# One factor for the two norms in front of a gated layer, and accumulators of their own per token tile in the last half of a down projection

## The chip, the cores and the metric

The kernel runs on one core of a Trainium2 chip. The metric is device time in microseconds, the median of several runs. TensorE is called PE (its weight loads are PEld), VectorE DVE, ScalarE ACT, GpSimd POOL; SyncE (SP) issues the transfers of the weights.

## What is computed

The input is 256 tokens of 1024 columns in float32. Two transformer blocks follow each other. The first is a mixer with sparse attention and an MLP with squared ReLU, and it ends with a norm; the second is a gated layer, a second mixer and a gated layer again. Cut to the part around the change:

```python
def rmsnorm(x, g):
    xf = x.astype(jnp.float32)
    y = xf * lax.rsqrt(jnp.mean(xf * xf, axis=-1, keepdims=True) + EPS)
    return (y * g.astype(jnp.float32)).astype(x.dtype)
...
x = rmsnorm(x, norm_final)                  # end of the first block
f = swiglu(rmsnorm_2(x, ffn1_pre_g[l]), ffn1_w_gate[l], ffn1_w_up[l], ffn1_w_down[l])
x = x + 0.5 * rmsnorm_2(f, ffn1_post_g[l])
```

So two norms stand right behind each other between the MLP's output (x2 in the kernel) and the products with the gate and up weights. The output of the first of them is also the residual of the gated layer.

## The kernel before

Every product runs in float32 as three matmuls of rounded parts: both operands are split into a rounded part (hi) and a residual (lo). The weights are streamed in units of 128x1024 values: SP transfers a unit (line 246), ACT writes hi (line 262), DVE writes lo = raw - hi (line 263). The split runs two units ahead of PE, the transfer five.

Products come in two kinds. `gemm_pair` (lines 358 to 376) computes a chunk of 256 features for all tokens: the features lie on the partitions, 16 pairs of a 512 column matmul (line 368) and a 256 column one (line 369) fill a pair of PSUM banks; ACT copies one half out (line 373), DVE adds the other (line 374) into a tile `sum`, of which there are two. `gemm_tok` (lines 287 to 335) computes 512 output columns (a column half) for two token tiles of 128 tokens, with the tokens on the partitions (lines 305 to 307), and calls `done` for each token tile when its last matmul has been issued. In the MLP and the gated layers PSUM holds three accumulator tiles of two banks each, and two banks for transposes; there, with `pair` set, the two token tiles of a chunk are the two banks of one accumulator tile. In the mixers every token tile has a tile of one bank.

The last column half of a down projection is called with `tail=2` (line 1160, in `down_post`): the last two units are first run for token tile 0 to the end, then for token tile 1, so that what follows for token tile 0 (a square with its sum, the gain on line 1123, a root, the new residual on line 1140) runs beside the matmuls of token tile 1.

`mlp` (lines 1008 to 1064) computes the MLP's chunks, then the two column halves of its output. `odone` (line 1036) adds the residual on line 1039, which gives x2, and squares it on ACT (`ssq`, line 432). The transposed parts of x2, times both gains by column (`gg`), are made by jobs (`jx`, lines 399 to 403) that go on between matmuls; the factor of the norm is left out of them and multiplied in later. Behind the column halves come the sum of the squares (line 1048), its mean, and an inverse root by Newton steps (lines 434 to 445) that gives rf; then xf = x2 * rf * gain (line 1057) in two passes, the squares of xf, a second mean and inverse root, and the product of both factors, rs (line 1063).

`ffn` (lines 1165 to 1187) spreads rs along the tokens (`along_free`, lines 538 to 551: two scalings of ones on line 547, matmuls on line 548, a copy to rsB on line 549), and multiplies rsB into each chunk of the gate product (line 1178) ahead of the SiLU (line 1179).

The order on PE, ACT and DVE is not that of the text: a planner with a timeline of its own lays it out when the program is built. SP and POOL work in the order of the text. The pools of `mlp` (`mlph`, `mlpt`) are given back at the end of the `with` block, and the gated layer's pools take their space.

Of the kernel before, what the change touches and what calls it, by code (L numbers as in the profile page):

```python
# [9 lines left out]
F32 = mybir.dt.float32  # L10
# [4 lines left out]
ALU = mybir.AluOpType  # L15
# [6 lines left out]
D = 1024  # L22
KT = 2
NEG = -1.0e30
EPS = 1e-6
# [184 lines left out]
class Prog:  # L210
# [76 lines left out]
    def gemm_tok(self, W, c, xh, xl, done, head=0, tail=0, mid=None, late=None, rate=1, delay=0, acc=None):  # L287

        nc = self.nc
        w = W.widths[c]
        if self.pair:
            ps = self.pacc.tile([128, 2, 512], F32, tag="acc", name="acc")
            ps = [ps[:, 0, :], ps[:, 1, :]]
        else:
            acc = acc or (lambda: self.pacc.tile([128, 512], F32, tag="acc", name="acc"))
            ps = [acc() for _ in range(2)]
        nu = len(W.off[c])

        def mm(kt, t):
            k, hi, lo = kt
            sl = slice(t * 128, t * 128 + 128)
            last = k == W.kt - 1
            nc.tensor.matmul(ps[t][:, :w], xh[:, k, sl], hi, start=(k == 0), stop=False)  # L305
            nc.tensor.matmul(ps[t][:, :w], xh[:, k, sl], lo, start=False, stop=False)  # L306
            nc.tensor.matmul(ps[t][:, :w], xl[:, k, sl], hi, start=False, stop=last)  # L307
            if last:
                done(t, ps[t][:, :w])

        held = []
        for u in range(nu):
            kts = self.load_unit(W, c, u)
            if u < head or u >= nu - tail:
                for kt in kts:
                    mm(kt, 0)
                    if u < head:
                        self.flush(rate)
                held += kts
                if u == head - 1 or u == nu - 1:  # L320
                    if u == head - 1 and mid:
                        mid()
                    for i, kt in enumerate(held):
                        mm(kt, 1)
                        if u < head:
                            self.flush(rate)
                        elif late:
                            late(len(held) - 1 - i)
                    held = []
                continue  # L330
            for kt in kts:
                for t in range(2):
                    mm(kt, t)
                if delay <= kt[0] < W.kt - 1:
                    self.flush(rate)
# [672 lines left out]
    def mlp(self, x1):  # L1008
        tc, nc, g = self.tc, self.nc, self.g
        s = self.small(2, "s1")  # L1010
        for t in range(2):
            self.ssq(s[:, t:t + 1], x1[:, t, :])
        r2 = self.small(2, "r1")
        self.mean_eps(r2, s)
        nc.vector.reciprocal(r2, r2)
        x2 = self.xp.tile([128, 2, D], F32, tag="x", name="x2")
        sq = self.small(4, "s2")
        gg = self.small(8, "gg")
        nc.vector.tensor_tensor(gg, g["norm_final"], g["ffn1_pre_g_2"], op=ALU.mult)
        with tc.tile_pool(name="mlph", bufs=1) as hp, tc.tile_pool(name="mlpt", bufs=2) as tp:  # L1020
            hT = [hp.tile([128, 32, 256], F32R, name="hT%d" % i) for i in range(2)]

            self.sump = tp

            def hdone(c):
                def f(p):
                    h = tp.tile([128, 2, 256], F32, tag="h", name="h")
                    nc.vector.scalar_tensor_tensor(h, p, 0.0, p, op0=ALU.max, op1=ALU.mult)
                    self.split_sb(h, hT, 2 * c)
                return f  # L1030
            for c in range(len(W_MI.widths)):
                self.gemm_pair(W_MI, c, self.x1T, hdone(c), delay=1, rate=2)
            xT = self.new_xT()
            jx = self.split_T(lambda t, k: x2[:, t, k * 128:k * 128 + 128], range(8), [0, 1], *xT, gg)

            def odone(c):
                def f(t, ps):
                    cs = slice(c * 512, c * 512 + 512)
                    nc.vector.scalar_tensor_tensor(x2[:, t, cs], ps, r2[:, t:t + 1], x1[:, t, cs], op0=ALU.mult,
                                                   op1=ALU.add)  # L1040
                    self.ssq(sq[:, 2 * c + t:2 * c + t + 1], x2[:, t, cs])
                return f
            for c in range(2):
                self.gemm_tok(W_MO, c, *hT, odone(c), delay=1, rate=2)
                self.later(*jx[4 * c:4 * c + 4])
        self.dump("x2", x2)
        ss = self.small(2, "s2b")
        nc.vector.tensor_tensor(ss, sq[:, 0:2], sq[:, 2:4], op=ALU.add)
        v = self.small(2, "vf")
        self.mean_eps(v, ss)  # L1050
        rf = self.small(2, "rf")
        self.newton_rsqrt(rf, v, 2, "rfn")
        gf = self.row_gain(0)
        xf = self.xp.tile([128, 2, D], F32, tag="x", name="xf")
        s = self.small(2, "sf")
        for t in range(2):
            nc.vector.scalar_tensor_tensor(xf[:, t, :], x2[:, t, :], rf[:, t:t + 1], gf, op0=ALU.mult, op1=ALU.mult)
            self.ssq(s[:, t:t + 1], xf[:, t, :])
        v2 = self.small(2, "vf2")
        self.mean_eps(v2, s)  # L1060
        rs = self.small(2, "rsf")
        self.newton_rsqrt(rs, v2, 2, "rsn")
        nc.vector.tensor_tensor(rs, rs, rf, op=ALU.mult)
        return xf, xT, rs

    def split_sb(self, h, hT, k):

# [508 lines left out]
```

## Time and profile before

| | us |
|---|---|
| median of 3 runs | 1151.42 |
| lowest and highest | 1150.39, 1152.96 |
| profiled execution | 1152.25 |
| its span, first to last instruction | 1150.5 |
| PE busy | 1114.8 (97%) |
| DVE busy | 769.6 (67%) |
| ACT busy | 573.0 (50%) |
| POOL busy | 137.0 (12%) |

Times in the rows are microseconds from the span's start. In a timeline a row is: start, duration, engine, line of the kernel, operation, written tile <- read tiles, shape, count, and in brackets the idle time of the engine just before it with what ended it. PE's rows are pipelined: a matmul starts before the one ahead of it has ended, so that what counts is the distance from start to start. The MLP's output projection ends near 414, the first gated layer runs from about 409 to 609, the last one to the end.

### The profile page before, as it was taken

What the parts mean: (1) busy time and instruction counts of PE and PEld (TensorE: products, weight loads), DVE (VectorE), ACT (ScalarE), POOL (GpSimd) and SP (SyncE); (2) the same over time, 40 slices, a digit from 0 to 9 for tenths busy, and PEclk for the clock granted to TensorE, in tenths of its full rate; (3) what the DMA queues carried; (4) which work ended last, traced back from release to release, by engine and by line L of the source; (5) the groups of instructions that cost most, each with busy time, mean ns of one, the idle gap of its engine ahead of it and who ended that gap; (6) DMA issues with size and microseconds to landing.
All of it is one profiled execution on the core that took longest, in us unless ns stands there. A gap on an engine that the chain in (4) does not pass through costs nothing.

```text
span 1150.5 us, 17641 instructions
## 1 busy us (share of the span) xinstructions
PE 1114.8 (97%) x6848; PEld 995.0 (86%) x6848; DVE 769.6 (67%) x1207; ACT 573.0 (50%) x854; POOL 137.0 (12%) x141
## 2 busy tenths in 40 slices
PE   8988999999999998999999999999999999999997
PEld 8877899888888877888878999889999987888885
DVE  6855776777754466776547686556779777777643
ACT  6424454465544455555445334544555555655552
POOL 1411220000000000000000675000323000000000
PEclk9998999999999998999999999999999999999999
DMA  8782114666555654555554655434545555555552
GB/s 295 250 193 94 63 53 143 201 185 198 185 193 175 202 174 153 183 183 188 196 178 146 209 179 167 166 129 143 174 148 167 159 190 178 186 189 189 183 183 74
DMA packets 55876, 196.91 MB, mean 171 GB/s; under 512 B 6700, under 2 KB 6972, under 8 KB 55536
## 3 DMA queue, kind: packets, MB, share of 16 engines
q1 hardware_dynamic: 52704, 186.44, 49.6%
q0 software_dynamic: 2800, 9.21, 3.2%
q8 instruction: 54, 0.88, 0.3%
q14 instruction: 30, 0.25, 0.1%
q10 hardware_dynamic: 288, 0.14, 0.0%
HBM read 192.84 MB, written 1.44 MB: 169 GB/s over the span
## 4 chain that ended last, share of the span: by engine, by line
PE 84%; POOL 5%; DMA 4%; DVE 4%; ACT 2%; issue 1%; DVEq 0%; SPq 0%; POOLq 0%; ACTq 0%
PE acc L368 19%; PE acc L369 10%; PE acc L305 9%; PE acc L306 9%; PE acc L307 9%; PE acc L349 6%; PE acc L351 6%; PE acc L352 6%; PE sm L835 2%; POOL sw L1255 2%; DMA sw<-qkT 2%; POOL qkT L1256 2%; DMA BT<-tvd 1%; PE o L868 1%; POOL qkT L1254 1%; DVE lo L263 1%
## 5 line engine op out<-in xcount | busy, mean ns | idle before, releaser
L263 DVE TENSOR_TENSOR lo<-raw,hi 128x1024 fp32r<-128x1024 f32 (+2 forms) x356 | 450.7, 1269 | 270.9 <-ACT hi L262 268.9
L262 ACT ACTIVATE hi<-raw 128x1024 fp32r<-128x1024 f32 (+2 forms) x356 | 371.1, 1044 | 439.1 <-issue 132.7
L368 PE MATMUL acc<-xs,hi 128*128 128x512 f32 x960 | 342.6, 401 | 6.2 <-DVE sum L374 6.0
L369 PE MATMUL acc<-xs,lo 128*128 128x256 f32 x960 | 270.1, 282 | 0.7 <-DVE lo L263 0.7
L368 PEld LDWEIGHTS acc<-xs,hi 128*128 128x128 f32 x960 | 181.9, 190 | 50.5 <-issue 4.7
L349 PE MATMUL acc<-xs,hi 128*128 128x256 f32 (+1 forms) x696 | 199.7, 288 | 0.3 <-ACT hi L262 0.3
L351 PE MATMUL acc<-xs,hi 128*128 128x256 f32 (+1 forms) x696 | 198.9, 287 | 0.0
L352 PE MATMUL acc<-xs,lo 128*128 128x256 f32 (+1 forms) x696 | 198.0, 287 | 0.1
L369 PEld LDWEIGHTS acc<-xs,lo 128*128 128x128 f32 x960 | 182.9, 191 | 1.3 <-DVE lo L263 1.0
L349 PEld LDWEIGHTS acc<-xs,hi 128*128 128x128 f32 (+1 forms) x696 | 133.4, 192 | 3.7 <-issue 2.5
L351 PEld LDWEIGHTS acc<-xs,hi 128*128 128x128 f32 (+1 forms) x696 | 133.7, 192 | 2.4 <-issue 2.0
L352 PEld LDWEIGHTS acc<-xs,lo 128*128 128x128 f32 (+1 forms) x696 | 132.9, 192 | 1.6 <-issue 1.0
L305 PE MATMUL acc<-hi,hT 128*128 128x512 f32 x304 | 118.7, 391 | 3.4 <-DVE f L1123 3.4
L306 PE MATMUL acc<-lo,hT 128*128 128x512 f32 x304 | 118.5, 390 | 0.0
L307 PE MATMUL acc<-hi,hT 128*128 128x512 f32 x304 | 118.0, 389 | 0.0
L305 PEld LDWEIGHTS acc<-hi,hT 128*128 128x128 f32 x304 | 57.1, 188 | 16.1 <-DVE f L1123 4.3
L307 PEld LDWEIGHTS acc<-hi,hT 128*128 128x128 f32 x304 | 57.1, 188 | 11.9
L306 PEld LDWEIGHTS acc<-lo,hT 128*128 128x128 f32 x304 | 57.1, 188 | 11.7
L305 PE MATMUL acc<-hi,xs 128*128 128x386 f32 (+1 forms) x128 | 48.6, 381 | 2.1 <-DVE xs L403 2.0
L306 PE MATMUL acc<-lo,xs 128*128 128x386 f32 (+1 forms) x128 | 48.2, 377 | 0.0
L307 PE MATMUL acc<-hi,xs 128*128 128x386 f32 (+1 forms) x128 | 47.3, 376 | 0.0
L374 DVE TENSOR_TENSOR sum<-acc,sum 128x512 f32<-128x512 f32 x60 | 41.1, 684 | 0.0
(419 smaller groups left out, 1388.2 us busy)
## 6 DMA issues: line engine op xcount, KB each, us to landing
raw<-in_w_in SPq DMA_DIRECT2D x100, 512.0 KB, 3.5
raw<-in_ffn_w_gate SPq DMA_DIRECT2D x44, 512.0 KB, 3.4
raw<-in_ffn_w_up SPq DMA_DIRECT2D x44, 512.0 KB, 3.4
raw<-in_ffn_w_down SPq DMA_DIRECT2D x44, 512.0 KB, 3.4
raw<-in_w_mlp_in SPq DMA_DIRECT2D x32, 512.0 KB, 3.5
raw<-in_w_mlp_out SPq DMA_DIRECT2D x32, 512.0 KB, 3.3
raw<-in_w_out SPq DMA_DIRECT2D x16, 512.0 KB, 3.4
raw<-in_w_in SPq DMA_DIRECT2D x16, 386.0 KB, 3.5
```

The costliest lines, as they stand in the source:

```text
L262: nc.scalar.activation(hi[:, :n * w], raw[:, :n * w], AF.Copy)
L263: nc.vector.tensor_tensor(lo[:, :n * w], raw[:, :n * w], hi[:, :n * w], op=ALU.subtract)
L305: nc.tensor.matmul(ps[t][:, :w], xh[:, k, sl], hi, start=(k == 0), stop=False)
L306: nc.tensor.matmul(ps[t][:, :w], xh[:, k, sl], lo, start=False, stop=False)
L307: nc.tensor.matmul(ps[t][:, :w], xl[:, k, sl], hi, start=False, stop=last)
L349: nc.tensor.matmul(o, hi[:, fs], xh[:, k, :], start=(k == 0 and f % 2 == 0), stop=False, skip_group_check=True)
L351: nc.tensor.matmul(o, hi[:, fs], xl[:, k, :], start=False, stop=False, skip_group_check=True)
L352: nc.tensor.matmul(o, lo[:, fs], xh[:, k, :], start=False, stop=last, skip_group_check=True)
L368: nc.tensor.matmul(ps[:, f, :, :], hi[:, fs], x.both[:, k, :, :], start=(k == 0), stop=False)
L369: nc.tensor.matmul(ps[:, f, 0, :], lo[:, fs], x.hi[:, k, :], start=False, stop=last)
L374: nc.vector.tensor_tensor(s, ps[:, :, 0, :], s, op=ALU.add)
L835: nc.tensor.matmul(ps[:, i, :], q[pr:pr + 64, U["fts"][i], t * 128:t * 128 + 128], kk, start=True, stop=True)
```

## The change

`gemm_tok` with `pair` and `tail` takes two accumulator tiles instead of one; each token tile then has the first bank of a tile of its own.

In `mlp` the row of gains is fetched ahead of the column halves. `odone` also multiplies x2 by the gain on POOL, into a new tile of the MLP's pool, and squares that product on ACT. Behind the column halves the sums of both kinds of squares give both factors: with v the mean of x2's squares plus EPS and w the mean of the product's squares, the product of the two old factors is one inverse root, of w + EPS * v. It comes first; rf, the inverse root of v, comes second and scales the product (in two passes on DVE, with a column of factors) to the residual that the gated layer adds at its end.

```diff
--- before.py
+++ after.py
@@ -291,8 +291,8 @@
         nc = self.nc
         w = W.widths[c]
         if self.pair:
-            ps = self.pacc.tile([128, 2, 512], F32, tag="acc", name="acc")
-            ps = [ps[:, 0, :], ps[:, 1, :]]
+            ps = [self.pacc.tile([128, 2, 512], F32, tag="acc", name="acc") for _ in range(2 if tail else 1)]
+            ps = [ps[0][:, 0, :], ps[1][:, 0, :] if tail else ps[0][:, 1, :]]
         else:
             acc = acc or (lambda: self.pacc.tile([128, 512], F32, tag="acc", name="acc"))
             ps = [acc() for _ in range(2)]
@@ -1036,32 +1036,38 @@
             def odone(c):
                 def f(t, ps):
                     cs = slice(c * 512, c * 512 + 512)
+                    i = 2 * c + t
                     nc.vector.scalar_tensor_tensor(x2[:, t, cs], ps, r2[:, t:t + 1], x1[:, t, cs], op0=ALU.mult,
                                                    op1=ALU.add)
-                    self.ssq(sq[:, 2 * c + t:2 * c + t + 1], x2[:, t, cs])
+                    nc.gpsimd.tensor_tensor(xf[:, t, cs], x2[:, t, cs], gf[:, cs], op=ALU.mult)
+                    self.ssq(sq[:, i:i + 1], x2[:, t, cs])
+                    self.ssq(sy[:, i:i + 1], xf[:, t, cs])
                 return f
+            gf = self.row_gain(0)
+            xf = hp.tile([128, 2, D], F32, name="xg")
+            sy = self.small(4, "s3")
             for c in range(2):
                 self.gemm_tok(W_MO, c, *hT, odone(c), delay=1, rate=2)
                 self.later(*jx[4 * c:4 * c + 4])
+
+
+            v = self.small(2, "vf")
+            nc.vector.tensor_tensor(v, sq[:, 0:2], sq[:, 2:4], op=ALU.add)
+            self.mean_eps(v, v)
+            v2 = self.small(2, "vf2")
+            nc.vector.tensor_tensor(v2, sy[:, 0:2], sy[:, 2:4], op=ALU.add)
+            w2 = self.small(2, "vf3")
+            nc.vector.tensor_scalar(w2, v, EPS, None, op0=ALU.mult)
+            nc.vector.scalar_tensor_tensor(v2, v2, 1.0 / D, w2, op0=ALU.mult, op1=ALU.add)
+            rs = self.small(2, "rsf")
+            self.newton_rsqrt(rs, v2, 2, "rsn")
+            rf = self.small(2, "rf")
+            self.newton_rsqrt(rf, v, 2, "rfn")
+            xo = self.xp.tile([128, 2, D], F32, tag="x", name="xf")
+            for t in range(2):
+                nc.vector.tensor_scalar(xo[:, t, :], xf[:, t, :], rf[:, t:t + 1], None, op0=ALU.mult)
         self.dump("x2", x2)
-        ss = self.small(2, "s2b")
-        nc.vector.tensor_tensor(ss, sq[:, 0:2], sq[:, 2:4], op=ALU.add)
-        v = self.small(2, "vf")
-        self.mean_eps(v, ss)
-        rf = self.small(2, "rf")
-        self.newton_rsqrt(rf, v, 2, "rfn")
-        gf = self.row_gain(0)
-        xf = self.xp.tile([128, 2, D], F32, tag="x", name="xf")
-        s = self.small(2, "sf")
-        for t in range(2):
-            nc.vector.scalar_tensor_tensor(xf[:, t, :], x2[:, t, :], rf[:, t:t + 1], gf, op0=ALU.mult, op1=ALU.mult)
-            self.ssq(s[:, t:t + 1], xf[:, t, :])
-        v2 = self.small(2, "vf2")
-        self.mean_eps(v2, s)
-        rs = self.small(2, "rsf")
-        self.newton_rsqrt(rs, v2, 2, "rsn")
-        nc.vector.tensor_tensor(rs, rs, rf, op=ALU.mult)
-        return xf, xT, rs
+        return xo, xT, rs
 
     def split_sb(self, h, hT, k):
 
```

## Rows read from the trace of the kernel before

**Rows 1.** Page: the span, and PE's busy time.
```profile
span 1150.5 us, 17641 instructions
...
PE 1114.8 (97%) x6848; PEld 995.0 (86%) x6848; DVE 769.6 (67%) x1207; ACT 573.0 (50%) x854; POOL 137.0 (12%) x141
```

**Rows 2.** PE's timeline at the start of the first gated layer.
```profile
416.77 0.39 PE L369 MATMUL acc<-xs,lo 128*128 128x256 f32 x1 [0.69 <-DVE lo L263]
...
428.13 0.28 PE L369 MATMUL acc<-xs,lo 128*128 128x256 f32 x1
...
429.99 0.50 PE L368 MATMUL acc<-xs,hi 128*128 128x512 f32 x1 [1.58 <-DVE sum L374]
...
441.70 0.28 PE L369 MATMUL acc<-xs,lo 128*128 128x256 f32 x1
...
446.39 0.77 PE L368 MATMUL acc<-xs,hi 128*128 128x512 f32 x1 [4.42 <-DVE sum L374]
...
452.27 0.39 PE L368 MATMUL acc<-xs,hi 128*128 128x512 f32 x1
...
452.62 0.40 PE L368 MATMUL acc<-xs,hi 128*128 128x512 f32 x1
```

**Rows 3.** Busy time by stretch; after the POOL columns granted clock, DMA share, GB/s.
```profile
450.00:452.00 2.00, 2.00 (x7) 1.69 (x7) 0.90 (x2) 0.33 (x1) 0.00 (x0) 0.50 0.00 0
```

**Rows 4.** DVE's timeline at the start of the first gated layer.
```profile
414.40 0.75 DVE L1039 SCALAR_TENSOR_TENSOR x<-acc,r,x 128x512 f32<-128x512 f32 x1 [0.22 <-PE acc L307]
...
415.49 1.23 DVE L263 TENSOR_TENSOR lo<-raw,hi 128x1024 fp32r<-128x1024 f32 x1 [0.34 <-ACT hi L262]
...
423.11 0.15 DVE L445 SCALAR_TENSOR_TENSOR rf<-rfn_t,rf 128x2 f32<-128x2 f32 x1
...
423.30 2.48 DVE L1057 SCALAR_TENSOR_TENSOR xf<-x,rf,row 128x1024 f32<-128x1024 f32 x2
...
433.63 0.16 DVE L1063 TENSOR_TENSOR rsf<-rsf,rf 128x2 f32<-128x2 f32 x1
...
435.24 0.48 DVE L547 TENSOR_SCALAR rt<-ones,rsf 128x128 f32<-128x128 f32 x2
...
439.81 0.42 DVE L549 COPY rsB<-tr 128x256 f32<-128x256 f32 x1 [1.67 <-PE tr L548]
```

**Rows 5.** ACT's timeline at the start of the first gated layer.
```profile
415.37 0.61 ACT L432 ACTIVATE junk<-x 128x512 bf16<-128x512 f32 x1
...
424.68 1.06 ACT L432 ACTIVATE junk<-xf 128x1024 bf16<-128x1024 f32 x1 [2.00 <-DVE xf L1057]
...
427.91 0.58 ACT L373 ACTIVATE sum<-acc 128x512 f32<-128x512 f32 x1
...
444.92 0.60 ACT L373 ACTIVATE sum<-acc 128x512 f32<-128x512 f32 x1
```

**Rows 6.** Timeline, last half of the first gated layer's down projection.
```profile
602.14 0.39 PE L307 MATMUL acc<-hi,hT 128*128 128x512 f32 x1
...
603.45 0.74 DVE L1123 SCALAR_TENSOR_TENSOR f<-acc,rsf,row 128x512 f32<-128x512 f32 x1
...
604.25 0.50 PE L305 MATMUL acc<-hi,hT 128*128 128x512 f32 x1 [1.73 <-DVE f L1123]
```

**Rows 7.** Timeline, last half of the last gated layer's down projection.
```profile
1138.56 0.39 PE L307 MATMUL acc<-hi,hT 128*128 128x512 f32 x1
...
1140.67 0.50 PE L305 MATMUL acc<-hi,hT 128*128 128x512 f32 x1 [1.72 <-DVE f L1123]
```

**Rows 8.** Timeline, last half of the mixer's output projection.
```profile
948.66 0.68 DVE L1121 TENSOR_TENSOR f<-acc,row 128x512 f32<-128x512 f32 x1
948.80 0.39 PE L306 MATMUL acc<-lo,mT 128*128 128x512 f32 x1
```

**Rows 9.** Timeline, POOL and DVE beside each other in the mixer.
```profile
858.70 1.29 POOL L1448 TENSOR_TENSOR qkm<-xc,y 128x512 f32<-128x512 f32 x1
...
858.85 1.16 DVE L443 TENSOR_TENSOR h_t<-h0r 128x4 f32<-128x4 f32 x1
```

## The prediction

> **What bounds the kernel now.** The page comes first: the span is 1150.5 us, and TensorE (PE) is busy for 97% of it [rows 1]. An edit can then only gain where PE stands still or runs slowly. So the second view is PE's own timeline at the two places that the change touches, the start of the first gated layer and the last column half of a gated layer's down projection; the reader is to look for the brackets, which give idle time and what ended it. The third view is the DVE and ACT timelines beside those stops.
>
> At the start of the gated layer PE stops three times [rows 2]. The first stop is a wait for a weight residual, 0.69 us at 416.77. The second runs from the end of the matmul that starts at 428.13 to 429.99. A pair of matmuls (512 and 256 columns) starts every 0.35 us at full pace (452.27, 452.62), of which the narrow one has a third, 0.12; so the stop is 429.99 - 428.13 - 0.12 = 1.74 us. The third is 446.39 - 441.70 - 0.12 = 4.57 us. Both wait for line 374, which empties an accumulator (each is named in the bracket of the row). Behind the third the granted clock is 0.50, the lower level of 1.2 GHz [rows 3]: nine pairs take 452.27 - 446.39 = 5.88 us where 9 x 0.35 = 3.15 would do, 2.73 us more. The second stop, shorter, left the clock at full speed.
>
> Why line 374 is late: a chunk's sum stays in one of two buffers until the norm's factor, spread along the tokens (rsB), has been multiplied into it; with both full, the third accumulator can't be emptied. The DVE timeline [rows 4] shows the chain of that factor: x2 is complete at 415.15, the first factor rf at 423.26, xf is written from 423.30 on in two passes, 2.48 together, the second factor is finished at 433.79 and rsB is copied at 439.81. The ACT timeline [rows 5] shows the first accumulator's copy (line 373) at 427.91, behind the squares of xf, and the third one's at 444.92, behind rsB, the table load and the SiLU.
>
> At the end of a down projection PE waits once more: the last matmul of token tile 0 starts at 602.14, the next, of token tile 1, at 604.25, released by line 1123, which reads token tile 0's accumulator [rows 6]. A matmul at full pace has 0.23 us, so 604.25 - 602.14 - 0.23 = 1.88 us. In the last layer the same stop is 1140.67 - 1138.56 - 0.23 = 1.88 us [rows 7]. The two accumulators are halves of one tile.
>
> **The change, part one: bank pairs per token tile.** Each token tile gets a tile of its own. Where that is so already, in the mixer's output projection, PE goes on: line 1121 reads token tile 0 from 948.66 on for 0.68 us, while a matmul of token tile 1 starts at 948.80 [rows 8]. So both stops go: 2 x 1.88 = 3.76 us. What could take their place: the third buffer is asked for by one more chunk, and its last reader is long done; in the first layer the next matmuls wait for transposes of token tile 1, whose chain begins at PE's last matmul and so moves along with it. In the last layer all that follows is that same chain and the output, so the gain reaches the end of the span. Bounds: 0 and 3.76; I take 3.76, since that row is the very case [rows 8].
>
> **Part two: the norms.** Removed from DVE are the two passes of line 1057 (2.48) and a product; from ACT two squares of 1024 columns. Added to POOL are four multiplications of 128x512; the same shape took 1.29 us there [rows 9]. Added to ACT are four squares of 512 columns, 0.61 us each against 1.06 for each of the two removed [rows 5]: 0.3 us more in all, two of the four in the first column half, where nothing waits for them; I cost them at nothing but their place in ACT's queue (below). Added to DVE are three tiny operations and two scalings of 128x1024 with a column of factors. The trace has that operation only at 128x128, 0.48 us for two [rows 4]; the same width in another operation is line 1057, 2.48 for two. I take 2.48, the row of the same width; the bounds are 0.48 and 2.48. The Trainium skill (VectorE: DVE Perf Modes, section on the perf-mode tier table) says that a scaling with one float32 source in SBUF can run at twice the pace; by its table I would estimate some 0.65 us each, and the sum below would be at most 0.45 us better, since the second stop would rather be gone. No row here shows that width.
>
> The path of the factor now is: x2 at 415.15, POOL 1.29, a square, sums, one inverse root, then rsB. The old path to rf had the square and the root already, and took until 423.26 with weight splits and transposed parts in between. I add POOL's 1.29 and, since two squares now queue on ACT, another 0.8 (0.61 and the reading of its sum): the factor is there at 425.4 instead of 433.79. The old distance from factor to rsB's copy was 439.81 - 433.79 = 6.0 us, much of it a place far down PE's queue; kept whole, the copy starts at 431.4. The second root and the scalings come beside or behind it on DVE.
>
> Does that remove the third stop? From rsB's copy to PE's restart it took 446.39 - 439.81 = 6.6 us. PE gets to that place at 440.9 to 441.8 (below), so the copy has to start by 434.3 to 435.2. With 431.4 there are 3 us to spare: the stop (4.57) and the slow pairs behind it (2.73) go, 7.30 us together.
>
> The second stop: the first accumulator's copy no longer stands behind squares that wait for xf, and could start 3.2 us earlier (the first of these squares started at 424.68). But the new tile for x2 times gain lies in the MLP's pool, whose space the gated layer takes over. If its first buffers wait for that whole pool, they wait for the scalings: 425.4 + 2.48 = 427.9, which is where the copy was. So this stop is shortened to nothing or stays where it ends now.
>
> Against that stands a hold between POOL and DVE. A DVE operation on 128x4, of some 0.16 us elsewhere (line 445 in rows 4), took 1.16 us at 858.85, beside a POOL multiplication that began at 858.70 and took 1.29: it ended when POOL had ended [rows 9]. Here POOL would begin its last multiplication at some 415.2, when x2 is there, just ahead of the residual split at 415.49 [rows 4], for which PE is already waiting. POOL is done at 416.5; the split, if it too has no more than some 0.15 behind it by then, ends its 1.23 us at 417.57 instead of at 416.72, and PE's first stop grows by 0.85 us. It can be nothing, if the split gets in first, and 1.29 at most. The Trainium skill (SBUF — State Buffer, section on who interferes with whom) says that a vector instruction with two SBUF inputs and a POOL instruction that reads SBUF exclude each other for the whole length of the one that began first. By that rule the loss is the full 0.85 us and no later split is spared if it meets POOL; without any hold the sum would be 0.85 us better. The trace agrees with the rule.
>
> Both together: PE arrives at the second stop 0.85 us later, at 429.10. If the stop still ends at 429.99, nothing is won or lost (0.85 + 0.89 = 1.74); if it is gone, 1.74 - 0.85 = 0.89 is won. I take the middle, 0.45. The three other multiplications fall where DVE's splits run ahead of PE's use; they cost nothing unless PE uses up the two units of lead. On POOL's queue only the next row of gains stands behind them, which is not used until the down projection.
>
> **Sum.** 3.76 + 7.30 + 0.45 = 11.5 us. The profiled execution took 1152.25 us (the span and 1.75 around it): 1140.75. It stands 0.83 above the median of 1151.42; from the median the sum gives 1139.9. I forecast 1140.3. About 0.2%, 2.3 us, is what a measurement of this kernel can tell from no change.
>
> **Rivals.**
> *A late factor.* DVE has less idle time in this stage than its mean shows, since splits now come without the pause that xf's squares made, and PE's queue is in a fixed order. If rsB's copy starts at 437, the third stop stays at some 2 us: 1142.3 with full clock; if the clock falls too, 1145.0. For it: the inverse root was stretched to over twice its work by splits. Against: 3 us to spare. Chance 0.15.
> *The first stage gains nothing*, since another wait takes over all of it: only the tails gain, 1152.25 - 3.76 = 1148.5. Against: the buffers do fill for want of rsB alone. Chance 0.06.
> *The separate tiles don't remove the wait*: 1152.25 - 7.75 = 1144.5. The mixer speaks against it [rows 8]. Chance 0.03.
> *Slower.* The first accumulator's copy waits for the scalings, and these, with the second root, are put far back in DVE's order. PE then stops at 429.10 until 2.1 us after their end (the old distance from that copy to the restart). Before, the stage lost 1.74 + 4.57 + 2.73 = 9.04, and the tails win 3.76; with 0.85 for POOL and 2.73 for a fallen clock, the stop has to exceed 9.2 us, so the scalings must end after 436.2 to make the kernel slower. At 440 it is 3.8 us slower: 1156. I expect them at 427.9. Chance 0.03. Between this and the others lies no change, 0.03.
>
> **The numbers.** The forecast has 0.70, by itself 1137 to 1142.5: below, both stops of the stage and the first one gone and a run as low as the fastest before; above, the second stop full, POOL held twice. The range takes in the late factor up to a fallen clock: 1136.8 to 1145.5, which leaves out less than 2 in 10. Faster: 0.70 + 0.15 + 0.06 + 0.03 = 0.94.
>
> **What would show it.** Right: in both down projections token tile 1's first matmul starts 0.23 us behind token tile 0's last; rsB's copy starts before 435; no stop over 1 us between 430 and 460 and no granted clock of 0.50 there; the split beside POOL's fourth multiplication takes over 2 us. Wrong: a stop of several us on line 374 again, line 373 waiting for the scalings, or PE standing before the product that spreads the factor.

## The result, and the profile after

| | before | after |
|---|---|---|
| median, us (lowest, highest; runs) | 1150.97 (1150.39, 1152.96; 4) | 1141.0 (1138.22, 1143.17; 4) |
| profiled execution | 1152.25 | 1140.78 |
| its span | 1150.5 | 1139.0 |

The changed kernel takes 0.9909 of the time, with a 95% interval of 0.9884 to 0.9934. The forecast was 1140.3, in a range of 1136.8 to 1145.5.

The page of the changed kernel, against [rows 1]:

```profile
span 1139.0 us, 17655 instructions
...
PE 1112.4 (98%) x6848; PEld 993.6 (87%) x6848; DVE 766.9 (67%) x1208; ACT 573.3 (50%) x858; POOL 143.8 (13%) x145
```

PE's busy time fell by 2.4 us, the span of the profiled execution by 11.5 (the medians differ by 10.0): most of what went was standing still. PE's timeline at the start of the first gated layer, against [rows 2]:

```profile
416.16 0.39 PE L369 MATMUL acc<-xs,lo 128*128 128x256 f32 x1 [1.57 <-DVE lo L263]
...
427.51 0.28 PE L369 MATMUL acc<-xs,lo 128*128 128x256 f32 x1
427.63 0.61 PE L548 MATMUL tr<-ident,rt 128*128 128x128 f32 x4
429.30 0.50 PE L368 MATMUL acc<-xs,hi 128*128 128x512 f32 x1 [1.06 <-DVE sum L374]
```

The first stop grew from 0.69 to 1.57 us. The second has 1.06 in its bracket where it had 1.58, but the product that spreads the factor (line 548) now stands inside it; that is nearly the whole difference, for from start to start the stop is 1.67 us where it was 1.74. The third is gone: the busy time by stretch (length, PE busy, granted clock, DMA share, GB/s) shows PE busy throughout at full clock, where [rows 3] had 0.50.

```profile
430.00:450.00 20.00, 20.00 (x115) 1.00 0.64 210
```

DVE's timeline there, against [rows 4]:

```profile
414.00 3.24 DVE L263 TENSOR_TENSOR lo<-raw,hi 128x1024 fp32r<-128x1024 f32 x2 [0.34 <-ACT hi L262]
...
423.02 1.42 DVE L1068 TENSOR_SCALAR xf<-xg,rf 128x1024 f32<-128x1024 f32 x2
424.35 0.15 DVE L445 SCALAR_TENSOR_TENSOR rsf<-rsn_t,rsf 128x2 f32<-128x2 f32 x1
424.54 0.48 DVE L547 TENSOR_SCALAR rt<-ones,rsf 128x128 f32<-128x128 f32 x2
427.42 1.23 DVE L263 TENSOR_TENSOR lo<-raw,hi 128x1024 fp32r<-128x1024 f32 x1 [2.40 <-ACT hi L262]
428.56 0.68 DVE L374 TENSOR_TENSOR sum<-acc,sum 128x512 f32<-128x512 f32 x1
429.16 0.42 DVE L549 COPY rsB<-tr 128x256 f32<-128x256 f32 x1
```

The factor is finished at 424.5 instead of 433.79, and rsB's copy starts at 429.16 instead of 439.81; of both, 1.50 us come from an earlier x2, which is not the change's (the table below). In the first row two residual splits take 3.24 us together where one takes 1.23: POOL's last product runs beside them (POOL's timeline):

```profile
413.74 1.29 POOL L1042 TENSOR_TENSOR xg<-x,row 128x512 f32<-128x512 f32 x1 [3.80 <-DVE x L1040]
```

ACT's timeline at the second stop, against [rows 5], has the first accumulator's copy (line 373) right behind a weight split:

```profile
426.32 1.06 ACT L262 ACTIVATE hi<-raw 128x1024 fp32r<-128x1024 f32 x1 [4.26 <-PE acc L368]
427.29 0.58 ACT L373 ACTIVATE sum<-acc 128x512 f32<-128x512 f32 x1
```

The two down projections (PE's and DVE's timeline, against [rows 6, 7]; line 1129 is line 1123 of before):

```profile
593.77 0.39 PE L307 MATMUL acc<-hi,hT 128*128 128x512 f32 x1
594.00 0.39 PE L305 MATMUL acc<-hi,hT 128*128 128x512 f32 x1
...
595.09 0.74 DVE L1129 SCALAR_TENSOR_TENSOR f<-acc,rsf,row 128x512 f32<-128x512 f32 x1
597.87 0.74 DVE L1129 SCALAR_TENSOR_TENSOR f<-acc,rsf,row 128x512 f32<-128x512 f32 x1
...
1130.43 0.74 DVE L1129 SCALAR_TENSOR_TENSOR f<-acc,n_r,row 128x512 f32<-128x512 f32 x1
1133.21 0.74 DVE L1129 SCALAR_TENSOR_TENSOR f<-acc,n_r,row 128x512 f32<-128x512 f32 x1
```

Token tile 1 starts 0.23 us behind token tile 0's last matmul, with no bracket. The two starts of line 1129 lie 2.78 us apart in both layers; before they lay 4.84 and 4.81 apart.

Cut at five instructions that both kernels have, the two spans differ like this (us):

| from ... to | before | after | gained |
|---|---|---|---|
| start ... x2 of token tile 0, last column half (409.32; 407.82) | 409.32 | 407.82 | 1.50 |
| ... first down projection, f of token tile 0 | 194.13 | 187.27 | 6.86 |
| ... f of token tile 1 | 4.84 | 2.78 | 2.06 |
| ... last gated layer, f of token tile 0 | 531.58 | 532.56 | -0.98 |
| ... f of token tile 1 | 4.81 | 2.78 | 2.03 |
| ... end | 5.8 | 5.8 | 0.0 |

The second, third and fifth rows are where the change is: 10.95 us. The first lies ahead of it: the transfer from tvd to BT (line 596, at about 71 us), for which PE stands, took 16.92 us in the one execution and 15.15 in the other. The loss in the fourth row is behind the second mixer's end, where the clock stayed at 0.50 for longer (last section). Neither can be laid to a part of the change by these runs, and they partly cancel.

### The profile page after: what moved, and what is told of

It reads as the page before. It is cut to its first block, busy times and chain, and to the rows that moved or that the text cites. A ratio compares the mean times of both kernels' runs of the same rounds, so it can differ in the third digit from the quotient of the medians.

```text
span 1139.0 us, 17655 instructions
## 1 busy us (share of the span) xinstructions
PE 1112.4 (98%) x6848; PEld 993.6 (87%) x6848; DVE 766.9 (67%) x1208; ACT 573.3 (50%) x858; POOL 143.8 (13%) x145
## 4 chain that ended last, share of the span: by engine, by line
PE 85%; POOL 5%; DMA 4%; DVE 4%; ACT 1%; issue 1%; DVEq 0%; SPq 0%; POOLq 0%; ACTq 0%
PE acc L368 20%; PE acc L369 10%; PE acc L307 9%; PE acc L306 9%; PE acc L305 9%; PE acc L349 6%; PE acc L351 6%; PE acc L352 6%; PE sm L835 2%; POOL sw L1261 2%; DMA sw<-qkT 2%; POOL qkT L1262 2%; POOL qkT L1260 1%; PE o L868 1%; DVE lo L263 1%; DMA BT<-tvd 1%
```

## The experiments

The kernels are named by the first part of their label, e1 and so on. Each ratio is against runs of the kernel before on the same chip.

**Each part alone.** The first kernel (e1) is the kernel before with the separate tiles, as in the diff; the second (e2) is the changed kernel with the same lines the other way round.

```diff
-            ps = self.pacc.tile([128, 2, 512], F32, tag="acc", name="acc")
-            ps = [ps[:, 0, :], ps[:, 1, :]]
+            ps = [self.pacc.tile([128, 2, 512], F32, tag="acc", name="acc") for _ in range(2 if tail else 1)]
+            ps = [ps[0][:, 0, :], ps[1][:, 0, :] if tail else ps[0][:, 1, :]]
```

> The kernel before with the separate accumulator tiles alone. Theory (the stop in the down projections is a wait on a shared tile): both stops of 1.88 us are gone, token tile 1's first matmul starts 0.23 us behind token tile 0's last, the start of the first gated layer keeps its three stops (0.7, 1.7, 4.6 us) and its half clock, and the time falls by 4.1 us (2 x 1.88, and 0.15 each for the slow first matmul behind a stop), a ratio of 0.9964. Rival (PE must wait for DVE's read whatever the tile): both stops stay and the time doesn't move. Second rival (the gains of the two parts depend on each other): less than 3 us.

> The change with the shared accumulator tile put back. Theory: the start of the first gated layer is as in the changed kernel (a first stop of 1.6 us, a second of 1.1, no third, no half clock), the two stops of 1.88 us in the down projections are back, and the time is 6.9 us below the kernel before, a ratio of 0.9940. Rival (the planner's new order costs something later, so that the norms by themselves give less): the stage gains the same, and one to two of its 6.9 us are lost in the mixer and the last layer.

Measured: the tiles alone 0.9947 of the time before (0.9929 to 0.9965), the norms alone 0.9956 (0.9939 to 0.9974). The two gains, 0.53% and 0.44%, add up to 0.97%; together they measured 0.91%. The tiles gave some 2 us more than their forecast (0.9964) and the norms some 2 us less than theirs (0.9940); both forecasts lie just inside the intervals. The norms' rival, a loss in the mixer and the last layer, would fit the time, but their profile shows no such loss: from f of token tile 1 to f of token tile 0 in the last layer it takes 531.55 us, and before 531.58. DVE's timeline and the busy time by stretch of the first kernel:

```profile
606.48 0.74 DVE L1123 SCALAR_TENSOR_TENSOR f<-acc,rsf,row 128x512 f32<-128x512 f32 x1
609.26 0.74 DVE L1123 SCALAR_TENSOR_TENSOR f<-acc,rsf,row 128x512 f32<-128x512 f32 x1
```

```profile
450.00:452.00 2.00, 2.00 (x7) 0.50 0.12 47
452.00:454.00 2.00, 2.00 (x8) 0.50 0.00 0
```

Both tail stops are gone (2.78 us again) and the start of the gated layer is as it was, low clock included: from x2 to f (of token tile 0, the second row of the table) it takes 193.81 us, against 194.13. With the norms alone it is the other way round: 187.22 us from x2 to f, and the tail's stop is back (DVE's timeline, 4.80 apart):

```profile
597.77 0.75 DVE L1129 SCALAR_TENSOR_TENSOR f<-acc,rsf,row 128x512 f32<-128x512 f32 x1
602.57 0.74 DVE L1129 SCALAR_TENSOR_TENSOR f<-acc,rsf,row 128x512 f32<-128x512 f32 x1
```

So each part does its own share in its own place, and neither needs the other.

**POOL's hold on DVE.** In e3 the last of the four products of x2 and the gain goes to DVE.

```diff
-                    nc.gpsimd.tensor_tensor(xf[:, t, cs], x2[:, t, cs], gf[:, cs], op=ALU.mult)
+                    eng = nc.vector if i == 3 else nc.gpsimd
+                    eng.tensor_tensor(xf[:, t, cs], x2[:, t, cs], gf[:, cs], op=ALU.mult)
```

> The change with the fourth product (last column half, token tile 1) on DVE instead of POOL. Theory (POOL's product holds DVE's split): the split of the weights next to it takes 1.23 us again instead of 2.1, and PE's first stop is 0.7 us instead of 1.57. Rival (the first stop grew because ACT has the additional squares in its queue): the first stop stays at 1.4 to 1.6 us. The factor comes at about the same time in both; the total changes by under 1 us, which one look can't show.

One run took 1142.62 us. DVE's timeline has the split at its own length, with the product behind it:

```profile
415.54 1.23 DVE L263 TENSOR_TENSOR lo<-raw,hi 128x1024 fp32r<-128x1024 f32 x1 [0.34 <-ACT hi L262]
416.68 0.68 DVE L1043 TENSOR_TENSOR xg<-x,row 128x512 f32<-128x512 f32 x1
```

PE's first stop is 0.69 us again (PE's timeline), with the additional squares still on ACT, so that rival fell:

```profile
416.82 0.39 PE L369 MATMUL acc<-xs,lo 128*128 128x256 f32 x1 [0.69 <-DVE lo L263]
```

From x2 to f it takes 186.39 us, 0.88 less than in the changed kernel. The hold is real and costs what the stop grew by. The whole time, from one run, can't show 0.9 us.

**Separate tiles in the MLP's output as well.** e4 is the changed kernel with a tile of its own for each token tile also in the last column half of the MLP's output. In the changed kernel 13 pairs of the gate product stand between the last matmul of token tile 0 and the last three of token tile 1 (the expectation below has 15); in e4 these three run right behind, and x2 of token tile 1 starts 0.67 us behind token tile 0's instead of 5.08.

```diff
-    def gemm_tok(self, W, c, xh, xl, done, head=0, tail=0, mid=None, late=None, rate=1, delay=0, acc=None):
+    def gemm_tok(self, W, c, xh, xl, done, head=0, tail=0, mid=None, late=None, rate=1, delay=0, acc=None, two=False):
...
-            ps = [self.pacc.tile([128, 2, 512], F32, tag="acc", name="acc") for _ in range(2 if tail else 1)]
-            ps = [ps[0][:, 0, :], ps[1][:, 0, :] if tail else ps[0][:, 1, :]]
+            ps = [self.pacc.tile([128, 2, 512], F32, tag="acc", name="acc") for _ in range(2 if tail or two else 1)]
+            ps = [ps[0][:, 0, :], ps[1][:, 0, :] if tail or two else ps[0][:, 1, :]]
...
-                self.gemm_tok(W_MO, c, *hT, odone(c), delay=1, rate=2)
+                self.gemm_tok(W_MO, c, *hT, odone(c), delay=1, rate=2, two=c == 1)
```

> The change, and separate accumulator tiles also in the last column half of the MLP's output. Theory (the first two stops that are left come from token tile 1's last three matmuls, which the shared tile puts off by 4.5 us behind 15 pairs of the gate product): these three run right behind token tile 0's, x2 is complete 4 us earlier against the first pairs of the gate product, the first stop (1.57) and the second (1.1) are gone, and the time is 2.6 us below the changed kernel, near 1138.4, a ratio of 0.989 to the kernel before. Rival (three accumulators are too few: the gate product then waits for a bank pair): one or both stops stay or a new one of 1 to 2 us comes at the start of the gate product, and the time is that of the changed kernel or above.

Measured: 1139.82 us, 0.9886 (0.9862 to 0.9910). x2 to f takes 185.36 us, 1.91 less than in the changed kernel. The first stop is gone; the second is what it was (PE's timeline):

```profile
425.20 0.61 PE L548 MATMUL tr<-ident,rt 128*128 128x128 f32 x4
426.87 0.50 PE L368 MATMUL acc<-xs,hi 128*128 128x512 f32 x1 [1.06 <-DVE sum L374]
```

So the half of the theory about the second stop fell: earlier transposes don't touch it.

**A late factor.** Multiplications by one on POOL, each waiting for the one before it, hold the factor back in the changed kernel: twelve in e7, as in the diff, and thirty-six in e8.

```diff
             self.newton_rsqrt(rs, v2, 2, "rsn")
+            for _ in range(12):
+                nc.gpsimd.tensor_tensor(rs, rs, self.ones[:, 0:2], op=ALU.mult)
```

> The changed kernel with the factor rs made late: twelve multiplications by one on POOL, each waiting for the one before, stand between the inverse root and the product that spreads it. It asks whether the factor's time alone made the third stop of the kernel before. A tiny POOL operation has no row like it; between 0.1 us (its 128x8 memset) and 0.3 us each, rsB's copy moves from 429.2 to 430.4 to 432.8. Theory, the two full sum buffers wait for rsB and nothing else: that is ahead of the limit of 435, so there is no third stop, and the time stays within 0.3 us at the start of the gated layer. Rival, every us of a later factor costs PE some of it: a third stop or a longer second one of 0.5 us or more.

> The same with thirty-six multiplications: rsB's copy moves by 3.6 to 10.8 us, or further where the product's place in TensorE's queue moves behind. Theory: the third stop is back as soon as the copy starts behind 435, and lasts as long as the copy is behind that, within 1 us (a copy at 440, as in the kernel before, gives 4 to 5.5 us); with a stop of 4 us or more the granted clock falls to 0.50 behind it, and the stage is longer by the stop and by about 2.7 us. Copy ahead of 435: no stop. Rival, the third stop and the low clock came from the two passes that wrote the residual and their squares, and not from the factor's time: no stop over 1.5 us on line 374 however late the copy is, up to 440, and the clock stays at full.

With twelve, one run took 1138.13 us. POOL's and PE's timelines, and the row of rsB's copy (count, durations in ns, first and last start):

```profile
426.58 4.12 POOL L1065 TENSOR_TENSOR rsf<-rsf,ones 128x2 f32<-128x2 f32 x12 [9.56 <-DVE rsf L445]
...
431.30 0.50 PE L368 MATMUL acc<-xs,hi 128*128 128x512 f32 x1 [1.51 <-DVE sum L374]
```

```profile
L549 DVE COPY rsB<-tr x1: 424/424/424, 435.4 to 435.4; 128x256 f32<-128x256 f32 x1
```

The copy is 6.2 us later. This execution has x2 2.0 us later than the changed kernel's, so on that one's scale the copy is at 433.4, ahead of the limit. There is no third stop: the third accumulator's addition starts at 441.16, and PE takes up the next pair at 442.95 without a wait (DVE's and PE's timelines).

```profile
441.16 0.69 DVE L374 TENSOR_TENSOR sum<-acc,sum 128x512 f32<-128x512 f32 x1
...
442.95 0.39 PE L368 MATMUL acc<-xs,hi 128*128 128x512 f32 x1
```

With thirty-six PE restarts 0.84 us behind the start of this addition (445.43, 446.27), so here about 1 us was to spare. The bracket of the second is 1.51 instead of 1.06, yet PE restarts 21.48 us behind x2 in both kernels (431.30 - 409.82 and 429.30 - 407.82): the product has moved behind the stop, and the 0.45 us that it filled are idle now. So the rival's longer stop is in the bracket, but it does not put off the restart; what the late factor costs here is the product's 0.45 us, which now stand between pairs, a little more than the 0.3 that the theory allowed.

With thirty-six, one run took 1147.12 us. PE's timeline, DVE's row of the copy, and the stretch behind (columns as above):

```profile
441.58 0.28 PE L369 MATMUL acc<-xs,lo 128*128 128x256 f32 x1
446.27 0.76 PE L368 MATMUL acc<-xs,hi 128*128 128x512 f32 x1 [4.41 <-DVE sum L374]
```

```profile
440.11 0.41 DVE L549 COPY rsB<-tr 128x256 f32<-128x256 f32 x1
```

```profile
446.00:448.00 2.00, 1.73 (x5) 0.50 0.50 201
448.00:450.00 2.00, 2.00 (x7) 0.50 0.00 0
```

With the copy at 440.11 the third stop is back, 446.27 - 441.58 - 0.12 = 4.57 us, to the hundredth what it was before, and the clock falls to 0.50 behind it. x2 to f takes 192.71 us, 5.44 more than in the changed kernel, where the theory had the stop and 2.7, together 7.3. Fifteen pairs behind the restart a pair starts 7.17 us later after x2 than in the changed kernel: 4.57 for the stop, 0.45 for the product between pairs, 2.2 for the slow pairs. Behind that the layer gives 1.7 back, since its pairs start 0.347 us apart instead of 0.353 (last section). Nothing else of the old path is in this kernel: neither the two passes nor their squares. POOL's chain does not hold DVE either: the four splits beside it take 1.22 or 1.23 us. The theory's rule had 440.1 - 435 = 5.1 us within 1, for the stop. So it is the factor's time alone that made the third stop and the slow pairs, and as long as the copy is ahead of the limit nothing is lost but the 0.45 us of a product that stands between pairs.

**What holds the second stop?** First, in e6, a fifth buffer for the parts of a weight unit, on e4.

```diff
-            self.wr = pool("wr", DMA_AHEAD - SPLIT_AHEAD + 1)
-            self.wh = pool("wh", SPLIT_AHEAD + 2)
-            self.wl = pool("wl", SPLIT_AHEAD + 2)
+            self.wr = pool("wr", DMA_AHEAD - SPLIT_AHEAD)
+            self.wh = pool("wh", SPLIT_AHEAD + 3)
+            self.wl = pool("wl", SPLIT_AHEAD + 3)
```

> The version with separate tiles also in the MLP's output, and with five buffers instead of four for the rounded part and for the residual of a weight unit (and three instead of four for raw units, which pays for the space). It asks what holds the second stop (1.06 us in the changed kernel and in the version without this edit, where the rounded part of the unit behind the first accumulator's end waits 4.3 and 5.3 us for TensorE to release a buffer, and residual and line 374 queue behind it). Theory, the buffers hold it: with a fifth, that wait falls to under 3 us or stands ahead of an earlier unit, line 374 no longer has a residual right ahead of it, and the second stop falls below 0.5 us; the sum of all stops at the start of the gated layer falls by 0.6 to 1.1 us. Rival, the order holds it: line 373 can't start before the accumulator is complete, and copy, addition and restart alone take the four pairs that stand between (1.4 us) and 1 us more, whatever the splits do; the stop stays at 0.8 to 1.1. The time of the whole kernel is not the test, since more lead and fewer raw units change the order everywhere.

Measured: 1148.47 us, 0.9971 (0.9948 to 0.9994). PE's and ACT's timelines:

```profile
434.52 0.60 PE L548 MATMUL tr<-ident,rt 128*128 128x128 f32 x4
436.16 0.50 PE L368 MATMUL acc<-xs,hi 128*128 128x512 f32 x1 [1.03 <-DVE sum L374]
```

```profile
433.19 1.06 ACT L262 ACTIVATE hi<-raw 128x1024 fp32r<-128x1024 f32 x1 [5.42 <-PE acc L368]
434.15 0.58 ACT L373 ACTIVATE sum<-acc 128x512 f32<-128x512 f32 x1
```

The stop stays at 1.03, and a split that has waited 5.42 us still stands right ahead of line 373. The theory of the buffers fell, as far as this kernel can show it, which also has a raw buffer less. The kernel is some 9 us slower than e4, and its x2 is 9.17 us later: the loss lies ahead of this stage, and whether the missing raw buffer or the changed order makes it was not tried.

The copy behind that split is left as a suspect. In e9, again on e4, the split of the eighth unit stands behind line 373 on ACT and line 374 on DVE.

```diff
-        nc.scalar.activation(s, ps[:, :, 1, :], AF.Copy)
-        nc.vector.tensor_tensor(s, ps[:, :, 0, :], s, op=ALU.add)
+        a = nc.scalar.activation(s, ps[:, :, 1, :], AF.Copy)
+        d = nc.vector.tensor_tensor(s, ps[:, :, 0, :], s, op=ALU.add)
+        if W is W_G1 and c == 0:
+            self.mark1 = a, d
...
-            with self.held(self.n_split in self.hold):
+            with self.held(self.n_split in self.hold), ExitStack() as es:
+                if self.n_split - self.units.index((W_G1, 0, 0)) in (7,):
+                    for m in self.mark1:
+                        es.enter_context(self.tc.issue_after(m.ins))
```

> The version with separate tiles also in the MLP's output; on ACT and DVE the split of the eighth unit of the first gated layer now stands behind line 373 and line 374 of the first accumulator, instead of ahead of them; nothing else is asked for. It asks again what holds the second stop, after a fifth buffer left it at 1.03 us and a late factor, with which the product that spreads it stands elsewhere, showed it at 1.51, as long as in the kernel before. Theory, the copy and the addition stand behind that unit's split in two queues: the first accumulator is complete about four pairs ahead of the stop, at 424.3 in the trace of the version without this edit, the copy then starts at 424.3 instead of 424.86, the addition at 424.9 instead of 426.13, and TensorE, which restarts 0.74 us behind the addition's start, goes on at 425.6, which is when it gets there: the second stop of 1.06 us falls below 0.3. Rival, the chain of copy, addition and restart is itself too long or the split that is moved is needed at once: the stop stays at 0.7 to 1.1 us, or a wait for the residual (line 263) of as much takes its place. The whole time: 0 to 1 us below the 1139.8 of the version without the edit, less than the runs can tell apart; against the kernel before 0.988.

Measured: 1140.39 us, 0.9901 (0.9863 to 0.9939). ACT's, DVE's and PE's timelines (lines 376, 377 and 371 are 373, 374 and 368):

```profile
428.71 0.60 ACT L376 ACTIVATE sum<-acc 128x512 f32<-128x512 f32 x1 [5.48 <-PE acc L372]
429.20 2.00 ACT L265 ACTIVATE hi<-raw 128x1024 fp32r<-128x1024 f32 x2
```

```profile
429.34 0.69 DVE L377 TENSOR_TENSOR sum<-acc,sum 128x512 f32<-128x512 f32 x1 [3.00 <-ACT sum L376]
```

```profile
429.85 0.61 PE L553 MATMUL tr<-ident,rt 128*128 128x128 f32 x4
430.21 0.48 PE L371 MATMUL acc<-xs,hi 128*128 128x512 f32 x1
```

The copy now waits for the accumulator itself, and PE runs from the product into the next pair without a stop. x2 to f takes 184.01 us, 1.35 less than without the edit. So the second stop was an order in two queues: a split that PE did not need yet, ahead of a copy that it did.

The three versions with all of the change and four buffers (the changed kernel, e4, e9) can't be told apart by their times: 0.9909, 0.9886 and 0.9901, with intervals that overlap. By the stage's length in single profiles, 187.27, 185.36 and 184.01 us, e9 is the best of them.

## Why the prediction was right, and where it was not

The direction, the size and the two places were right: 11.5 us were forecast, and the two profiles differ by 11.5, the medians by 10.0. Of the profiles' difference, 10.95 are the change's.

**Tails.** Forecast 3.76, measured 2.06 + 2.03 = 4.09. The separate tiles do what the mixer's row showed, nothing took the stop's place, and e1 has the whole of it without the norms. Each is 0.15 to 0.18 us more than the stop alone, for the matmuls behind the stop were slower too: in the first layer the first of them is 0.35 us ahead of the next (604.25, 604.60) instead of 0.23, and the ten behind go at 0.232 instead of 0.226.

**The factor.** Forecast 425.4 for the factor and 431.4 for rsB's copy; measured 424.5 and 429.16, but with x2 1.50 us earlier. Counted from x2 of token tile 0, the factor took 16.7 us where 16.1 were forecast, and the copy 21.3 where 22.1 were. So the factor was slower than forecast. The distance from it to the copy, which I kept whole at 6.0 us, is 4.66, since the planner put the product earlier in PE's queue, and this more than made up for it.

**Third stop and slow pairs.** Forecast 7.30, and both are gone. e8 shows that the factor's time was the cause: with the copy at 440.11 both are back. The rival of a late factor was thus a real mechanism. Counted from x2, its limit was forecast at 25.0 to 25.9 us; e7, with a copy at 25.6 and about 1 us to spare, puts it near 26.5, and e8's copy at 31.8 is behind it. The rival did not happen because the changed kernel's copy, at 21.3, came some 5 us ahead of the limit.

**POOL's hold.** Forecast 0.85, measured 0.88 (1.57 - 0.69), and e3 takes it away. The rule of the Trainium skill (SBUF — State Buffer, section on who interferes with whom) by which the two exclude each other for the whole instruction agrees with both rows: the split beside POOL ends late, the split without it takes 1.23.

**The second stop: the step that failed.** It read: "the first accumulator's copy no longer stands behind squares that wait for xf, and could start 3.2 us earlier". It could not. PE works on several chunks in turn, and the first accumulator's last pair comes only four pairs, 1.4 us, ahead of the stop, in PE's order of before as of after; in e9, where nothing stands ahead of the copy, it waits for that pair until 428.71, 1.1 us before PE gets to the product. I had read what stood ahead of the copy in ACT's queue and not when its input was complete. The other half, that the copy might wait for the scalings since the pool's space is handed on, did not show either: they end at 424.44, and the copy is at 427.29 behind a split. The stop from start to start, 1.74 us before, is 429.30 - 427.51 - 0.12 = 1.67 now. So neither of the two ends forecast for it came, gone or at the old time: PE restarts 21.48 us behind x2 instead of 20.67, put off by about as much as POOL's hold had put off PE. What the change did gain here is that the product's 0.45 us lie inside the stop; before, the product stood between two pairs, which started 0.80 us apart for it (438.93, 439.73) instead of 0.35 (PE's timeline):

```profile
439.16 0.60 PE L548 MATMUL tr<-ident,rt 128*128 128x128 f32 x4
```

So in place of +0.45 net the second stop and the hold give 0.07 + 0.45 - 0.88 = -0.36, and the stage 7.30 - 0.36 = 6.94; 6.86 were measured.

**The scalings.** I took 2.48 us for the two, from the row of the same width; they took 1.42, 0.71 each. The Trainium skill's table (VectorE: DVE Perf Modes, section on the perf-mode tier table), from which I had estimated 0.65, was nearer. It made no difference, since nothing waited for them: the 0.45 us that I attached to quicker scalings was attached to the wrong wait.

**What cancelled.** 0.9 us too much in the stage, 0.3 too little in the tails, and 1.50 - 0.98 that the two executions differ by elsewhere. The exact agreement of the sums is luck; that the size came out is not, since the two largest terms were right.

## What to carry to other kernels

A value that every buffer waits for has a latest time: work it out from PE's restart backwards, and a change that moves the value from behind that time to ahead of it wins the whole stop and the low clock behind it, and little more for being earlier still (here 0.45 us, where the product that spreads it fell into another stop). Before saying that an instruction "could start earlier" when its queue is cleared, look up when its input is complete. Beside a stop, look at what stands right ahead of the instruction that ends it on each queue: here one split, moved behind the copy and the addition, removed a stop that an earlier factor, earlier transposes and a fifth buffer (with a raw buffer less) had all left alone.

## What the runs showed of the hardware that was not expected

**Two paces at the same granted clock.** With clock 1.00 and no stop, pairs of the gated layer start 0.3533 us apart in one execution and 0.3467 in another, near the same place of the layer. PE's timeline of the changed kernel, eighteen pairs apart (6.36 us):

```profile
499.71 0.40 PE L368 MATMUL acc<-xs,hi 128*128 128x512 f32 x1
...
506.07 0.40 PE L368 MATMUL acc<-xs,hi 128*128 128x512 f32 x1
```

and of the kernel with twelve multiplications (6.24 us):

```profile
499.81 0.39 PE L368 MATMUL acc<-xs,hi 128*128 128x512 f32 x1
...
506.05 0.39 PE L368 MATMUL acc<-xs,hi 128*128 128x512 f32 x1
```

It is not the change's: in the MLP ahead of it, 18 pairs take 6.24 us before (280.25 to 286.49) and 6.36 in e1 (280.36 to 286.72), which has the same code there. Behind the second stop of the first gated layer only e7, and e8 behind its third, have the quicker pace, so that the other kernels' lengths from x2 to f can be compared. The pace also changes within an execution: in the changed kernel it is 0.347 ahead of the second stop and 0.353 behind it, in e8 0.347 behind the third. Over the 352 pairs of a gated layer's two products, 0.0066 us each make 2.3 us; the runs of one kernel differ by a few us. It also accounts for the length in e7, whose way from x2 to f is 185.68 us, 1.59 less than the changed kernel's: 352 - 48 pairs behind the restart by 0.0066 are 2.0, less the 0.45 of the product that moved out of the stop. What sets the pace stays open.

**The low clock behind the second mixer.** Behind the stop at that mixer's end, the sum of (1 - clock) times length is 1.7 us in the profiles of before, e1, e3 and e6, and 3.4 in those of the changed kernel, e2, e4, e7, e8 and e9. e3 and e6 have both parts of the change and not the longer low clock, so the change does not make it by itself. It goes with the -0.98 us in the table above: from the mixer's last read of an accumulator (line 1121 of before) to f of token tile 0 the first four take 188.85 to 189.19 us and the others 189.85 to 190.25, but for e7 (187.81), whose pairs there have the quicker pace. What decides it stays open.

**Tiny POOL operations.** Multiplications of 128x2, each waiting for the one before, took 4.12 us for twelve and 13.46 for thirty-six, 0.34 to 0.37 us each, where I had put 0.1 to 0.3; a chain of operations of this size on DVE, the Newton steps, has a step every 0.19 to 0.20 us.
